# Both value projections of a layer as one matrix product of seven half-size products, with retention's values parked in memory

## The chip, the cores and the metric

The kernel runs on one core of one Trainium2 chip. The metric is device time in microseconds (us) of one execution; three runs of the kernel before took 1214.03 to 1214.75 us, median 1214.11 us.

## The reference

An encoder of two layers over 512 tokens of width 1024. Only the first half of a layer is touched by the change:

```python
h = rms_norm(x, attn_norm_g[l])
proj = h @ w_in[l]
rq, rk, rv, rg, dq, dk, dv = jnp.split(proj, split_at, axis=-1)      # each 512 x 512
ret = retention_bidir(rq, rk * RET_HEAD_DIM ** -0.5, rv, lg_f, lg_b)  # 8 heads
ret = rms_norm(ret, ret_norm_g[l]) * silu(rg)
da = diff_attention(norm(dq) * DIFF_HEAD_DIM ** -0.5, norm(dk), dv, lam, slopes)   # 4 heads
da = rms_norm(da, diff_norm_g[l]) * (1.0 - lam_init)
x = x + concat(ret, da) @ w_out[l]
h = rms_norm(x, ffn_norm_g[l])
x = x + (silu(h @ w_gate[l]) * (h @ w_up[l])) @ w_down[l]
```

The value projections are `dv` (for the differential attention) and `rv` (for retention): together 512 tokens by 1024 columns, summed over 1024 features.

## The kernel before, in words

**Number format.** All products run on 32-bit data rounded for TensorE, in three terms: each operand is a pair hi + lo, and `mm3` (L237 to L239) issues hi·hi, then the two mixed products into one accumulator. Weights come as chunks of 128x1024 (512 KB): SP loads a `raw` tile (three buffers), ScalarE rounds it to `hi` (L224), VectorE subtracts to `lo` (L230). `hi` and `lo` have three buffers each (`NHL`), so the cast of a chunk waits until the matmuls that read the chunk three places earlier are done.

**A layer.** `project_first` makes the first two query and two key tiles. The norm (`Norm.rows`, `Norm.cols`) sums squares on TensorE (L140, L141), makes `rstd` by Ln, Exp (L107), Square (L268) and two VectorE steps (L269, L270), and transposes it with four small matmuls (L301). Then come `project_dv` (four chunks, four token blocks, 96 matmuls of 128x512), the `qk_tile` work of the first tiles, and the four attention heads: scores (L452), a maximum (L456), Exp, the combination of both maps (L464, L465), four transposes on TensorE (L468), the rounding to `ah` (ScalarE, L471) and `al` (VectorE, L472), and the product with `dv` into `o`. Retention follows in `STEPS` (a: `prepare`, b: `scores`, n: `norm`, k, V, v, c: states, values, cross terms), and beside it `project_out`, whose first half copies each bank to an `x` tile on ScalarE (L802) and adds the old x to it with an accumulating DMA from the POOL queue (L803).

**Fillers.** What needs no head is a filler: `project_rk(1)`, `project_rq(1)`, `project_rv` (96 matmuls, its four values chunks in two passes over token halves), then rk and rq 2 and 3, then `project_out`. A "-" in `STEPS` takes one filler step. The instructions of each engine run in the order in which the scheduler of the framework put them, by its own model and by the extra dependencies in the code; an engine never overtakes within its own list.

**The feed-forward half** already uses seven half-size products, with 256 columns moving. It isn't touched.

Of the kernel before, what the change touches and what calls it, by code (L numbers as in the profile page):

```python
# [55 lines left out]
def encoder_kernel(ctx: ExitStack, tc: tile.TileContext, xT, xg, wfirst, wsingle, wvv, wout, wgu, wdn, wds, prm, lam, cst, outT):  # L56
# [63 lines left out]
    xscr = ctx.enter_context(tc.tile_pool(name="dpool", bufs=1, space=bass.MemoryType.DRAM)).tile([KT, P, T], F32, name="xscr")  # L120

# [150 lines left out]
    class Norm:  # L272
# [15 lines left out]
        def rows(self):  # L288
            ps = aux_bank()
            column_sums(ps, consts["ones_r"], self.sum)  # L290
# [58 lines left out]
    def layer(l, n1, h, x_src, first_raw):  # L349


        def project_first():
            banks = [b() for b in (acc_bank, acc_bank, sc_bank, sc_bank)]
            for c in range(4):
                w = [t.rearrange("p (k f) -> p k f", f=512) for t in split_chunk(*first_raw[c], first=l == 0 and c == 0)]
                for k in range(2):
                    kt = 2 * c + k
                    for i, ps in enumerate(banks):
                        mm3(ps, cut(w, slice(None), k, slice(i * P, (i + 1) * P)), h[kt], kt == 0, kt == KT - 1)
            return banks  # L360

        def project(name, m):
            w = [t.rearrange("p (k f) -> p k f", f=P) for t in chunk(wsingle[l, SINGLE.index((name, m))])]
            ps = acc_bank()
            for kt in range(KT):
                mm3(ps, cut(w, slice(None), kt), h[kt], kt == 0, kt == KT - 1)
            return ps

        first = project_first()
        if l == 0:  # L370
            nc.sync.dma_start(cst_sb, cst)
            round_ones()
        rstd = n1.rows()
        if l == 0:
            prepare_small()
        rstdc = n1.cols(rstd)
# [62 lines left out]
        def diff_head(hd, qs, ks, v):  # L439
            q, k = qs[hd], ks[hd]  # L440
            o = None
            for th in range(2):
                ah = tpool.tile([P, 4, C], F32R, tag="ah", name=nm("ah"), bufs=NAH)
                al = tpool.tile([P, 4, C], F32R, tag="ah", name=nm("al"), bufs=NAH)
                for i in (2 * th, 2 * th + 1):
                    z = small("z", 2)
                    pr = []
                    for m in range(2):
                        ps = sc_bank()
                        t = slice(i * P, (i + 1) * P)  # L450
                        for part in range(2):
                            nc.tensor.matmul(ps, q[m][:, t], k[m][part], start=part == 0, stop=part == 1)  # L452
# [23 lines left out]
                for j in range(4):  # L476
                    vv = cut(v[hd // 2][j], slice(None), slice((hd % 2) * P, (hd % 2 + 1) * P))
                    mm3(o[:, th * C : (th + 1) * C], vv, (ah[:, j, :], al[:, j, :]), j == 0, j == 3)
# [147 lines left out]
        def project_dv():  # L626
            banks = [b() for b in (out_bank, out_bank, acc_bank, acc_bank)]
            for c in range(4):
                w = [t.rearrange("p (k f) -> p k f", f=512) for t in chunk(wvv[l, 1, c])]
                for i in ((2, 3, 0, 1) if c == 3 else range(4)):  # L630
                    ps = banks[i]
                    for k in range(2):
                        kt = 2 * c + k
                        mm3(ps, cut(h[kt], slice(None), slice(i * P, (i + 1) * P)), cut(w, slice(None), k), kt == 0, kt == KT - 1)
                yield
            dv[:] = [[tuple(tpool.tile([P, 256], F32R, tag="dv", name=nm("dv"), bufs=16) for _ in range(2)) for _ in range(4)] for _ in range(2)]
            for i in (2, 3, 0, 1):
                ps = banks[i]
                for half in range(2):
                    f = slice(half * 256, (half + 1) * 256)  # L640
                    hi, lo = dv[half][i]
                    nc.scalar.activation(hi, ps[:, f], AF.Copy, scale=rstdc[:, i : i + 1])
                    nc.vector.scalar_tensor_tensor(lo, ps[:, f], rstdc[:, i : i + 1], f32(hi), op0=ALU.mult, op1=ALU.subtract)

        def project_rv():
            w = [None] * 4
            rvt = [[tpool.tile([P, 256], F32, tag="dv", name=nm("rv"), bufs=16) for _ in range(4)] for _ in range(2)]
            for th in range(2):
                banks = [acc_bank() for _ in range(2)]
                for n, c in enumerate(range(4) if th == 0 else range(3, -1, -1)):  # L650
                    if th == 0 or c == 0:
                        w[c] = [t.rearrange("p (k f) -> p k f", f=512) for t in chunk(wvv[l, 0, c])]
                    for i, ps in enumerate(banks):
                        tok = slice((2 * th + i) * P, (2 * th + i + 1) * P)
                        for k in range(2):
                            mm3(ps, cut(h[2 * c + k], slice(None), tok), cut(w[c], slice(None), k), n + k == 0, n + k == 4)
                    if n == 1:
                        yield
                for i, ps in enumerate(banks):
                    for half in range(2):  # L660
                        t = rvt[half][2 * th + i]
                        nc.scalar.activation(t, ps[:, half * 256 : (half + 1) * 256], AF.Copy, scale=rstdc[:, 2 * th + i : 2 * th + i + 1])
                        rv[half].append(t)
                yield
# [57 lines left out]
        us = []  # L722
        for ps in first:
            us.append(big("u"))
            nc.vector.tensor_tensor(us[-1], ps, rstd, op=ALU.mult)
        early_dv = project_dv()
        next(early_dv)
        for i, ((name, m), u) in enumerate(zip(FIRST, us)):
# [4 lines left out]
            next(early_dv, None)  # L733
# [45 lines left out]
        def project_out(half, get, *then):  # L779
# [27 lines left out]

        fill = fillers(
# [396 lines left out]
```

## Time and profile before

| | us |
|---|---|
| median of three runs | 1214.11 |
| profiled execution, its own time | 1214.05 |
| its span in the trace | 1212.3 |
| TensorE busy in the span | 1208.1 |
| VectorE busy | 958.2 |
| ScalarE busy | 746.6 |
| POOL busy | 106.0 |

TensorE works from end to end at the full granted clock (1.00 in all slices). A matmul's listed duration is longer than its step, since they are pipelined; the distance of two starts is what a matmul costs. The value stage of layer 0 lies at about 28 to 52 us of the trace, the heads reach to about 172 us, retention to 250 us; layer 1 repeats this some 600 us later.

### The profile page before, as it was taken

The page shows a single profiled execution, that of the slowest core. Times are in us where ns is not written, and L with a number is a line of the kernel's source. Part 1 is how long each engine was busy: PE and PEld are TensorE (multiplying, and loading weights), DVE is VectorE, ACT ScalarE, POOL GpSimd, SP SyncE. Part 2 cuts the span into 40 slices and gives each one's busy share as a digit, 9 for nine tenths or more (in the row PEclk, how much of TensorE's full clock was granted, in tenths as well). Part 3 has the DMA queues.
Part 4 walks back from the last instruction along what each step waited for, and adds up shares of the span by engine and source line. Part 5 has one row for each costly group of instructions (what it writes and reads, how often), then busy time and mean ns, then how long its engine had stood idle before and what let it go on. Part 6 is the DMA issues. An engine that isn't in the chain of part 4 may idle for free.

```text
span 1212.3 us, 20100 instructions
## 1 busy us (share of the span) xinstructions
PE 1208.1 (100%) x7659; PEld 1081.4 (89%) x7659; DVE 958.2 (79%) x1585; ACT 746.6 (62%) x1300; POOL 106.0 (9%) x124
## 2 busy tenths in 40 slices
PE   9999999999999999999999999999999999999998
PEld 7888888788899999999888888887888999999997
DVE  6899867678978888886648997776789788898763
ACT  6877677565456556655548777774554565665541
POOL 1000001300011111110000000012000011111100
PEclk9999999999999999999999999999999999999999
DMA  7223225933176796782532232469132767867822
GB/s 269 87 79 83 75 92 140 232 98 105 65 169 163 176 215 153 181 220 84 170 113 78 81 80 67 115 151 242 54 122 78 178 145 190 208 160 181 202 79 96
DMA packets 72288, 165.92 MB, mean 137 GB/s; under 512 B 7168, under 2 KB 17664, under 8 KB 72192
## 3 DMA queue, kind: packets, MB, share of 16 engines
q1 hardware_dynamic: 54448, 133.52, 36.2%
q0 software_dynamic: 17312, 30.68, 15.5%
q8 instruction: 60, 0.98, 0.3%
q10 hardware_dynamic: 432, 0.44, 0.1%
q14 instruction: 36, 0.29, 0.1%
HBM read 153.34 MB, written 4.19 MB: 130 GB/s over the span
## 4 chain that ended last, share of the span: by engine, by line
PE 99%; DMA 0%; ACT 0%; DVE 0%; issue 0%
PE acc L945 23%; PE sc L945 17%; PE acc L237 11%; PE acc L238 11%; PE acc L239 11%; PE o L239 3%; PE o L238 3%; PE o L237 3%; PE sc L237 3%; PE sc L239 3%; PE sc L238 3%; PE sc L452 2%; PE sc L601 1%; PE aux L468 1%; PE o L545 1%; PE o L534 1%
## 5 line engine op out<-in xcount | busy, mean ns | idle before, releaser
L224 ACT CAST hi<-raw 128x1024 fp32r<-128x1024 f32 (+2 forms) x117 | 115.9, 994 | 122.5 <-PE acc L238 42.1
L230 DVE TENSOR_TENSOR lo<-raw,hi 128x1024 fp32r<-128x1024 f32 (+2 forms) x118 | 135.0, 1147 | 54.8 <-ACT hi L224 53.4
L239 PE MATMUL acc<-h,lo 128*128 128x512 f32 (+1 forms) x344 | 134.3, 390 | 0.0
L237 PE MATMUL acc<-h,hi 128*128 128x512 f32 (+1 forms) x344 | 134.1, 393 | 0.2
L238 PE MATMUL acc<-h,hi 128*128 128x512 f32 (+1 forms) x344 | 133.8, 389 | 0.0
L945 PE MATMUL acc<-hi,hi 128*128 128x256 f32 x432 | 122.6, 284 | 0.0
L945 PE MATMUL acc<-hi,lo 128*128 128x256 f32 x432 | 122.3, 283 | 0.0
L945 PE MATMUL acc<-lo,hi 128*128 128x256 f32 x432 | 122.3, 283 | 0.0
L902 DVE TENSOR_TENSOR lo<-s,hi 128x1024 fp32r<-128x1024 f32 (+1 forms) x78 | 88.7, 1137 | 32.7 <-ACT hi L901 32.5
L902 DVE TENSOR_TENSOR lo<-raw,hi 128x1024 fp32r<-128x1024 f32 (+1 forms) x78 | 88.8, 1139 | 31.0 <-ACT hi L901 27.2
L901 ACT CAST hi<-s 128x1024 fp32r<-128x1024 f32 (+1 forms) x78 | 76.6, 983 | 51.6 <-PE acc L945 37.2
L901 ACT CAST hi<-raw 128x1024 fp32r<-128x1024 f32 (+1 forms) x78 | 76.5, 981 | 39.0 <-PE acc L945 18.8
L945 PEld LDWEIGHTS acc<-lo,hi 128*128 128x128 f32 x432 | 82.9, 192 | 0.1
L945 PEld LDWEIGHTS acc<-hi,hi 128*128 128x128 f32 x432 | 82.9, 192 | 0.1
L945 PEld LDWEIGHTS acc<-hi,lo 128*128 128x128 f32 x432 | 82.9, 192 | 0.0
L923 POOL DMA_DIRECT2D s<-in_wgu x36 | 43.3, 1204 | 424.3 <-DMA s<-in_wgu 253.5
L237 PEld LDWEIGHTS acc<-h,hi 128*128 128x128 f32 x344 | 64.6, 188 | 14.3 <-PE o L239 0.6
L239 PEld LDWEIGHTS acc<-h,lo 128*128 128x128 f32 x344 | 64.7, 188 | 13.2
L238 PEld LDWEIGHTS acc<-h,hi 128*128 128x128 f32 x344 | 64.6, 188 | 13.2
L945 PE MATMUL sc<-b,s 128*128 128x256 f32 x480 | 69.4, 283 | 0.0
L945 PEld LDWEIGHTS sc<-b,s 128*128 128x128 f32 x480 | 62.8, 192 | 0.0
L945 PE MATMUL acc<-h,hi 128*128 128x256 f32 x288 | 53.7, 283 | 0.0
(282 smaller groups left out, 3530.1 us busy)
## 6 DMA issues: line engine op xcount, KB each, us to landing
s<-in_wgu SPq DMA_DIRECT2D x54, 512.0 KB, 5.4
s<-in_wgu POOLq DMA_DIRECT2D x36, 512.0 KB, 7.9
raw<-in_wgu SPq DMA_DIRECT2D x34, 512.0 KB, 5.2
raw<-in_wsingle SPq DMA_DIRECT2D x32, 512.0 KB, 3.5
raw<-in_wvv SPq DMA_DIRECT2D x18, 512.0 KB, 3.5
raw<-in_wgu SPq DMA_DIRECT2D x36, 256.0 KB, 3.9
s<-in_wds SPq DMA_DIRECT2D x24, 384.0 KB, 3.5
raw<-in_wout SPq DMA_DIRECT2D x16, 512.0 KB, 4.4
```

The costliest lines, as they stand in the source:

```text
L224: c = nc.scalar.copy(hi[:, s], raw[:, s])
L230: nc.vector.tensor_tensor(lo[:, s], raw[:, s], f32(hi[:, s]), op=ALU.subtract)
L237: first = nc.tensor.matmul(out, L[0], R[0], start=start, stop=False)
L238: nc.tensor.matmul(out, L[0], R[1], start=False, stop=False)
L239: nc.tensor.matmul(out, L[1], R[0], start=False, stop=stop)
L452: nc.tensor.matmul(ps, q[m][:, t], k[m][part], start=part == 0, stop=part == 1)
L468: nc.tensor.transpose(tp[:, j * P : (j + 1) * P], a[:, j * P : (j + 1) * P], ident)
L534: ins.append(nc.tensor.matmul(o[b, t], r[:, d, b], qw[:, t], start=False, stop=d == 0, skip_group_check=True).ins)
L901: last_cast[0] = nc.scalar.copy(hi, raw).ins.name
L902: last_split[0] = nc.vector.tensor_tensor(lo, raw, f32(hi), op=ALU.subtract).ins.name
L923: nc.gpsimd.dma_start(sums, blocks[:, 0::3], accum_op=ALU.add)
L945: mm = nc.tensor.matmul(ps[:, t], L[x1], R[x2], start=start and k + i == 0, stop=k == n // P - 1 and i == 2, skip_group_check=True)
```

## The change

`[dv|rv]` is treated as one product. Its three dimensions (features, tokens, the two groups of 512 columns) are halved, and seven products of halves take the place of eight. Each of the seven is two token blocks by four feature tiles by three terms: 24 matmuls of 128x512.

- The sums and differences of `h` (`first_sides`, `second_sides`, `last_sides`) are made by ScalarE and VectorE; the first are placed between `rsqrt` and `newton` of the norm. The sums of weights are made by accumulating DMAs from the POOL queue (`summed`, ten in a layer, 512 KB each), into two `sum` tiles and into `raw` tiles that SP has loaded.
- All seven products stand ahead of the heads and between the first `qk_tile` calls. `dv` stays in its tiles. `rv` goes to memory (`spilled`, four writes of 256 KB in a layer), and `load_values` brings it back in eight loads of 128 KB to the tiles of `dv`, which come free during the heads.
- `project_rv` is gone from the fillers, with four "-" of `STEPS`. `BEHIND` ties the rk and rq fillers 2 and 3 behind scores and products of the last head.
- The sums of squares of the norm are issued ahead of the last chunk of `project_first`.
- The first four x copies of `project_out`'s first half move from ScalarE to VectorE.

```diff
-STEPS = "a0 h - b0 - a1 b1 - - - - - - a2 - - a3 b2 !k0+k1+V0+v1+c0+c1+k2+k3 b3 n0 n1 - - - !V2+v3+c2+c3 n2 - - - n3"
+STEPS = "a0 h - b0 - a1 b1 - - a2 - - a3 b2 - - !k0+k1+V0+v1+c0+c1+k2+k3 b3 n0 n1 - - - !V2+v3+c2+c3 n2 - - - n3"
+BEHIND = {'rk2': 's3.0', 'rq2': 's3.1', 'rk3': 's3.3', 'rq3': 'o3.1'}
...
+        def rows(self, between=None):
+            if between is None:
+                self.sums()
+            ps = self.ps
             r = big("rstd", tag="rstd", bufs=1)
             rsqrt(r, ps, 1.0 / D)
+            if between:
+                between()
             newton(r, ps, 1.0 / D, big("nt"))
...
             for c in range(4):
+                if c == 3:
+                    n1.sums()
...
+        def first_sides():
+            for i, d in enumerate(sides):
+                d.update(b11=cut(h[i], slice(None), H1), b21=cut(h[i + 4], slice(None), H1), b22=cut(h[i + 4], slice(None), H2))
+                b1 = d["b1"] = scaled_x(i, "mix", NMIX)
+                nc.vector.tensor_tensor(b1[:, H1], b1[:, H1], b1[:, H2], op=ALU.subtract)
+                d["ta"] = [big(n, F32R, "mix", NMIX) for n in ("hi", "lo")]
+                d["t1"] = split_to(b1[:, H1], cut(d["ta"], slice(None), H1))
...
+            def summed(t, v, c):
+                nc.gpsimd.dma_start(t, wvv[l, v, c], accum_op=ALU.add)
...
+            def product(ps, r, left, start=False):
+                for c in range(2):
+                    w = [t.rearrange("p (k f) -> p k f", f=512) for t in left(c)]
+                    for i in range(2):
+                        for k in range(2):
+                            L, R = cut(sides[2 * c + k][r], slice(None), slice(i * P, (i + 1) * P)), cut(w, slice(None), k)
+                            for n, (x1, x2) in enumerate(((0, 0), (0, 1), (1, 0))):
+                                nc.tensor.matmul(ps[i], L[x1], R[x2], start=start and c + k + n == 0, stop=c + k == 2 and n == 2, skip_group_check=True)
...
+            def pair_sum(v, other, half):
+                def left(c):
+                    new = load_chunk(wvv[l, v, c])
+                    summed(new[0], other, 2 * half + c)
+                    return split_chunk(*new)
...
+            s1, s3 = pair_sum(0, 0, 1), pair_sum(0, 1, 0)
...
+            product(pa, "b11", loaded(1, 0), True)
+            for c in range(2):
+                nc.sync.dma_start(held[c], wvv[l, 0, c])
+                summed(held[c], 0, 2 + c)
+                summed(held[c], 1, c)
...
+            product(pb, "b21", loaded(1, 1), True)
...
+            product(pa, "t2", s2)
...
+            product(pb, "t1", s1, True)
+            last_sides()
...
+            product(pa, "t3", s3)
...
+            product(pb, "b22", s4)
...
+            product(pa, "t4", loaded(0, 1))
...
+        def load_values():
+            for half in range(2):
+                for i in range(4):
+                    t = tpool.tile([P, 256], F32, tag="dv", name=nm("rv"), bufs=16)
+                    nc.sync.dma_start(t, rvscr[l, i][:, half * 256 : (half + 1) * 256])
...
-                    nc.scalar.copy(x[m], ps[m])
+                    (nc.vector.tensor_copy if m < 4 else nc.scalar.copy)(x[m], ps[m])
...
-            [project_rk(1), project_rq(1), project_rv(), project_rk(2), project_rq(2), project_rk(3), project_rq(3), project_out(0, acc_bank, None, None, None)]
+            [project_rk(1), project_rq(1), project_rk(2), project_rq(2), project_rk(3), project_rq(3), project_out(0, acc_bank, None, None, None)]
```

**How the order moves, first place: TensorE at the norm of layer 0.** `aux` with `rstd` is the transpose of the norm, `o` and `acc` are accumulators of the value products; the second fence is the kernel after. Before, the sums end 36 matmuls ahead of the transposes, and the last of them are these:

```order
L239 MATMUL o_392<-hi_505,h_142 128x512
L237 MATMUL o_392<-hi_505,h_152 128x512
L238 MATMUL o_392<-lo_506,h_152 128x512
L239 MATMUL o_392<-hi_505,h_152 128x512
L301 MATMUL aux_376<-cst_sb,rstd_321 128x128 x4
L237 MATMUL acc_393<-hi_397,h_102 128x512
L238 MATMUL acc_393<-lo_398,h_102 128x512
```

After, the last matmul of the sums is L144:

```order
L144 MATMUL aux_286<-lo_288,ones_r 128x512
L708 MATMUL o_445<-hi_452,h_113 128x512
L708 MATMUL o_444<-hi_470,h_124 128x512
L708 MATMUL o_445<-hi_470,h_124 128x512
...
L708 MATMUL o_445<-lo_471,h_134 128x512
L708 MATMUL o_445<-hi_470,h_134 128x512
L311 MATMUL aux_368<-cst_sb,rstd_324 128x128 x4
L708 MATMUL acc_446<-hi_518,h_145 128x512
L708 MATMUL acc_446<-lo_519,h_145 128x512
```

Thirteen matmuls now stand between the sums and the transposes, and the accumulator `acc_446` right behind them is a bank of `project_first` that VectorE must have read.

**Second place: VectorE and POOL in the value stage of layer 0, after only** (before has no such rows). `raw_625` and `raw_729` share a buffer; they are the first chunk of the sum for product t1 and the second for t3. VectorE:

```order
L259 TENSOR_TENSOR lo_666<-b_328,hi_665 128x512
L233 TENSOR_TENSOR lo_629<-raw_625,hi_628 128x1024
L389 TENSOR_TENSOR dv_493<-part_508,dv_492 128x256
L259 TENSOR_TENSOR lo_600<-sq_597,hi_599 128x512
L259 TENSOR_TENSOR lo_672<-b_335,hi_671 128x512
```

POOL:

```order
L699 DMA raw_625<-in_wvv 128x1024
L699 DMA raw_644<-in_wvv 128x1024
L699 DMA sum_448<-in_wvv 128x1024
L699 DMA raw_710<-in_wvv 128x1024
L699 DMA sum_449<-in_wvv 128x1024
L699 DMA raw_729<-in_wvv 128x1024
```

Before, POOL had only fills of tiles up to the heads; after, ten accumulating loads stand there.

**Third place: TensorE at the end of the last head of layer 0.** `aux` are the four transposes of a combined map, `o` with `ah` and `al` the product with `dv`, `acc` the filler (before `project_rv`, after `project_rk(3)`). Before:

```order
L468 MATMUL aux_1598<-cst_sb,sc_1581 128x128 x4
L239 MATMUL acc_1989<-hi_1932,h_131 128x512
L237 MATMUL o_1526<-ah_1462,dv_619 128x256
L238 MATMUL o_1526<-al_1463,dv_619 128x256
...
L468 MATMUL aux_1659<-cst_sb,sc_1642 128x128 x4
L237 MATMUL acc_1988<-hi_2028,h_102 128x512
L238 MATMUL acc_1988<-lo_2029,h_102 128x512
L239 MATMUL acc_1988<-hi_2028,h_102 128x512
```

After:

```order
L242 MATMUL acc_2263<-h_176,lo_2260 128x512
L534 MATMUL aux_1760<-cst_sb,sc_1742 128x128 x4
L534 MATMUL aux_1839<-cst_sb,sc_1822 128x128 x4
L240 MATMUL o_1767<-ah_1703,dv_500 128x256
L241 MATMUL o_1767<-al_1704,dv_500 128x256
```

and VectorE at that place, after:

```order
L792 SCALAR_TENSOR_TENSOR rk_2256<-acc_2263,rstd_324 128x512
L526 RECIPROCAL rz_1894<-z_1879 128x2
L528 TENSOR_SCALAR c_1896<-rz_1894,prm_sb 128x1
L233 TENSOR_TENSOR lo_2566<-raw_2563,hi_2565 128x1024
L530 TENSOR_SCALAR sc_1890<-sc_1890,c_1896 128x512
L538 TENSOR_TENSOR al_1704<-aux_1760,ah_1703 128x4x128
L538 TENSOR_TENSOR al_1817<-aux_1839,ah_1816 128x4x128
```

No filler stands between the last transposes and the products that read them any more, and `al_1704` stands behind a chunk's `lo_2566`, whose `hi_2565` has the buffer that `acc_2263` reads.

## Rows read from the trace of the kernel before

**Rows 1.** The page: span, and busy time of each engine (share, instructions).

```profile
span 1212.3 us, 20100 instructions
...
PE 1208.1 (100%) x7659; PEld 1081.4 (89%) x7659; DVE 958.2 (79%) x1585; ACT 746.6 (62%) x1300; POOL 106.0 (9%) x124
```

**Rows 2.** Waits of TensorE: line, releaser, us in total, times, longest.

```profile
PE aux L118 <- PEq L1197: 0.8, 1, 0.8
```

**Rows 3.** Stretches: length and PE, PEld, DVE, ACT, POOL busy, clock, DMA share, GB/s.

```profile
20.00:40.00 20.00, 20.00 (x92) 16.53 (x91) 11.36 (x28) 9.27 (x16) 0.00 (x0) 1.00 0.36 117
40.00:60.00 20.00, 20.00 (x89) 16.26 (x88) 18.31 (x29) 19.38 (x34) 0.00 (x0) 1.00 0.34 106
60.00:80.00 20.00, 19.96 (x92) 15.87 (x91) 19.74 (x43) 14.93 (x32) 0.00 (x0) 1.00 0.26 79
80.00:100.00 20.00, 20.00 (x107) 16.98 (x106) 19.83 (x41) 15.90 (x30) 3.00 (x5) 1.00 0.25 67
...
160.00:180.00 20.00, 20.00 (x109) 17.19 (x108) 14.51 (x26) 14.35 (x28) 0.00 (x0) 1.00 0.35 105
180.00:200.00 20.00, 20.00 (x102) 16.84 (x101) 16.53 (x25) 16.39 (x28) 2.09 (x4) 1.00 0.48 127
```

**Rows 4.** TensorE at the norm of layer 0: start, duration, line, tiles.

```profile
27.79 0.39 PE L141 MATMUL aux<-lo,ones_r 128*128 128x512 f32 x1
28.02 0.39 PE L237 MATMUL o<-hi,h 128*128 128x512 f32 x1
...
33.26 0.39 PE L239 MATMUL o<-hi,h 128*128 128x512 f32 x1
```

**Rows 5.** VectorE at the same place, the last step of the norm.

```profile
31.29 0.69 DVE L270 SCALAR_TENSOR_TENSOR rstd<-nt,rstd 128x512 f32<-128x512 f32 x1
```

**Rows 6.** Groups by shape: count, busy us, mean ns of one, idle before it.

```profile
L230 DVE TENSOR_TENSOR lo<-raw,hi 128x1024 fp32r<-128x1024 f32 x94 | 114.5, 1220 | 49.5 <-ACT hi L224 48.2 <-PE aux L141 0.5
L224 ACT CAST hi<-raw 128x1024 fp32r<-128x1024 f32 x94 | 98.5, 1050 | 100.3 <-PE acc L238 39.3 <-PE sc L238 38.6 <-PE acc L239 8.7
L465 DVE SCALAR_TENSOR_TENSOR sc<-sc,rz,sc 128x512 f32<-128x512 f32 x32 | 23.9, 746 | 0.5
L472 DVE TENSOR_TENSOR al<-aux,ah 128x512 fp32r<-128x512 f32 x32 | 21.7, 684 | 0.5 <-ACT ah L471 0.4
L960 DVE TENSOR_TENSOR u<-u,acc 128x256 f32<-128x256 f32 x52 | 21.6, 416 | 10.7 <-PE acc L945 9.6 <-ACT b L895 0.8
L471 ACT CAST ah<-aux 128x512 fp32r<-128x512 f32 x32 | 18.4, 583 | 12.2 <-PE aux L468 12.2
L464 DVE TENSOR_SCALAR sc<-sc,c 128x512 f32<-128x512 f32 x32 | 15.4, 482 | 0.5
```

**Rows 7.** DMA issues of the whole span: queue, count, KB each, median us to landing.

```profile
s<-in_wgu SPq DMA_DIRECT2D x54, 512.0 KB, 5.4
s<-in_wgu POOLq DMA_DIRECT2D x36, 512.0 KB, 7.9
...
raw<-in_wvv SPq DMA_DIRECT2D x18, 512.0 KB, 3.5
...
s<-in_wds POOLq DMA_DIRECT2D x16, 384.0 KB, 5.9
```

**Rows 8.** The same for the stretch 200 to 260 us, where DMA is busiest.

```profile
s<-in_wgu POOLq DMA_DIRECT2D x3, 512.0 KB, 9.3
```

**Rows 9.** TensorE at the end of the last head.

```profile
164.96 0.60 PE L468 MATMUL aux<-cst_sb,sc 128*128 128x128 f32 x4
165.31 0.47 PE L237 MATMUL acc<-hi,h 128*128 128x512 f32 x1
...
169.94 0.27 PE L237 MATMUL o<-ah,dv 128*128 128x256 f32 x1
170.06 0.28 PE L238 MATMUL o<-al,dv 128*128 128x256 f32 x1
```

**Rows 10.** VectorE there: the rounding of those transposes.

```profile
166.44 0.68 DVE L472 TENSOR_TENSOR al<-aux,ah 128x512 fp32r<-128x512 f32 x1
```

**Rows 11.** One line: the x copies of `project_out` (duration ns min/median/max, then first and last start).

```profile
L802 ACT COPY x<-acc x16: 565/579/591, 206.2 to 841.1; 128x512 f32<-128x512 f32 x16
```

More of the change, by code (lines that the diff above doesn't have):

```diff
@@ L365, in project, with split_to @@
             for kt in range(KT):
-                mm3(ps, cut(w, slice(None), kt), h[kt], kt == 0, kt == KT - 1)
-            return ps
+                i = mm3(ps, cut(w, slice(None), kt), h[kt], kt == 0, kt == KT - 1)
+                behind = BEHIND.get(name + str(m))
+                if behind and kt == 0:
+                    tc.add_manual_dep(i, marks[behind], order, reason="behind the heads")
+            return ps
+        def split_to(src, dst):
+            hi, lo = dst
+            nc.scalar.copy(hi, src)
+            nc.vector.tensor_tensor(lo, src, f32(hi), op=ALU.subtract)
+            return hi, lo
@@ L369, in layer @@
+        if l == 0:
+            round_ones()
         first = project_first()
@@ L371, in layer @@
             nc.sync.dma_start(cst_sb, cst)
-            round_ones()
-        rstd = n1.rows()
+        rstd = n1.rows(first_sides)
+        us = []
+        for ps in first:
+            us.append(big("u"))
+            nc.vector.tensor_tensor(us[-1], ps, rstd, op=ALU.mult)
+        rstdc = n1.cols(rstd)
+        second_sides()
         if l == 0:
             prepare_small()
-        rstdc = n1.cols(rstd)
         lg, nlgb, lamn, gq, gd, wk, rs = (consts[k] for k in ("lg", "nlgb", "lamn", "gq", "gd", "wk", "rs"))
@@ L624, in layer, with project_values, loaded, s2 @@
         rks, rqs, gates = [], [], []
[L626 to L638, printed above, removed]
+        def project_values():
+            pa, pb = [out_bank() for _ in range(2)], [acc_bank() for _ in range(2)]
+            held = [tpool.tile([P, 1024], F32, tag="ah", name=nm("sum"), bufs=NAH) for _ in range(2)]
+            def summed(t, v, c):
[8 more added lines that the diff above has]
+                                nc.tensor.matmul(ps[i], L[x1], R[x2], start=start and c + k + n == 0, stop=c + k == 2 and n == 2, skip_group_check=True)
+            def loaded(v, half):
+                return lambda c: chunk(wvv[l, v, 2 * half + c])
+            def s2(c):
+                parts = split_chunk(held[c], 1024, 1)
+                summed(held[c], 1, 2 + c)
+                return parts
+            def s4(c):
+                return split_chunk(held[c], 1024, 1)
+            def pair_sum(v, other, half):
[3 more added lines that the diff above has]
+                    return split_chunk(*new)
+                return left
+            s1, s3 = pair_sum(0, 0, 1), pair_sum(0, 1, 0)
+            def col(t, i):
+                return t[:, i : i + 1]
+            def kept(i, t):
@@ L639, in project_dv @@
                 for half in range(2):
                     f = slice(half * 256, (half + 1) * 256)
[L641 to L664, printed above, removed]
@@ L721, in layer @@
         q, k = [None] * 4, [None] * 4
[L722 to L727, printed above, removed]
+        rstdn = small("rstdn", 4)
+        nc.vector.tensor_scalar(rstdn, rstdc, -1.0, None, op0=ALU.mult)
+        values_ahead = project_values()
+        for _ in range(3):
+            next(values_ahead)
         for i, ((name, m), u) in enumerate(zip(FIRST, us)):
@@ L1114, in encoder_kernel @@
             raws = [load_chunk(wfirst[l, c]) for c in range(4)]
-        n, h = layer(l, n, h, xT if l == 0 else xscr, raws)
+        n, h, x = layer(l, n, h, x, xT if l == 0 else xscr, raws)
 def _constants():
```

84 lines of the change are left out of this document (70 added, 14 removed).

## The prediction, made before the changed kernel ran

> **What bounds the kernel now.** I read the page first, then the waits of TensorE, then the stretches, then single rows at the places where the change moves work. The page says that TensorE is busy 1208.1 of 1212.3 us, VectorE 79% and ScalarE 62% [rows 1]. The list of waits has one entry for TensorE, 0.8 us at the start [rows 2], and the stretches show it 20.00 of 20 us busy nearly everywhere, at granted clock 1.00 [rows 3]. So the end is set by the count of TensorE's work alone, and nothing else costs anything today. That has two sides: each matmul that goes is worth its full step, and each wait that the change puts into TensorE's list costs its full length, as there is no idle time that it could take the place of. Second, VectorE is not idle where it matters: 18.31 of 20 us from 40 to 60, 19.74 and 19.83 from 60 to 100 [rows 3]. It has slack at 20 to 40 (11.36) and from 160 on (14.51). A wait that VectorE meets in the value stage is therefore handed to the heads.
>
> **What it removes.** A value projection is 4 chunks x 2 feature tiles x 4 token blocks x 3 terms = 96 matmuls, two of them 192 in a layer; seven products are 7 x 24 = 168. In two layers 48 matmuls of 128x512 go. Their step: 23 matmuls lie between the starts 28.02 and 33.26, so 0.228 us [rows 4]. 48 x 0.228 = 10.9 us, all of it on the path. No other TensorE work changes in count.
>
> **What it adds off TensorE.** Counted over the program, VectorE gets 10 more instructions of 128x1024, 8 of 128x512 and 8 x copies, 12 of three operands with 512, and 48 of 128x256. At 1.220, 0.684, 0.746 and 0.416 us [rows 6] and 0.48 to 0.68 for a copy that has no row on this engine (between L464 and L472), that is 12.2 + 5.5 + 4.6 + 9.0 + 20.0 = 51 us, 25 in a layer. In the value stage the room is 20 - 11.36 + 20 - 18.31 = 10.3 us [rows 3], plus what `project_rv` leaves in the heads (five casts' `lo`, 6.1 us a layer). Twenty accumulating DMAs come to POOL, which is idle there. The spills and reloads of rv go by SP: 8 loads of 128 KB, needed only at about 215 us, long after head 1 frees their tiles; I cost them at nothing, since a landing of a few us is hidden behind heads 2 and 3, and without that cover one landing, 3.5 to 5.4 us [rows 7], would show.
>
> **A, the value stage of layer 0.** First the norm. From the last matmul of the sums (27.79) to the end of `rstd` (31.29 + 0.69 = 31.98) took 4.2 us [rows 4, 5], hidden behind 36 matmuls. After, 13 stand there: 0.23 + 13 x 0.228 = 3.2 us. ScalarE now has a chunk's cast within the chain (up to 1.05 us [rows 6]), so the chain is 4.2 to 5.2 us and the wait 1.0 to 2.0; I take 1.5. Right behind the transposes, `acc_446` needs VectorE to have read `project_first`'s banks, and VectorE does a `lo` of 1.22 and two reads of 0.68 after `rstd`, against 0.4 us of transposes; and by `lo_580` VectorE has some 11 to 12 us of work from `rstd` on, TensorE 39 matmuls and the transposes, 9.3 us. Together a backlog of 0 to 3 us; I take 2.0. Last, product t3: `raw_729` may be loaded only when `lo_629` has read its buffer, then POOL adds to it, then ScalarE casts it. A load is 3.5 us, the accumulating one 5.9 (384 KB, quiet) to 7.9 [rows 7], the cast 1.05: 10.5 to 12.5 us. TensorE has 37 matmuls between the first use of `lo_629` and that of `raw_729`'s `hi`, 8.4 us, and `lo_629` is finished shortly before its use: a wait of 2 to 4 us, none if its accumulating load lands as a plain one does (3.5). I take 3.0, nearer to the quiet end as the DMA share here is 0.36 [rows 3]. A = 6.5 us (0 to 9).
>
> For such loads the Trainium skill ("SBUF — State Buffer", section "SBUF: two separate sides") warns that a DMA issued from GpSimd has its descriptors written by GpSimd, that some instructions of VectorE keep it from writing them, and advises the other queues. The trace agrees in sign: 7.9 us from POOL against 5.4 from SP for the same 512 KB of `in_wgu` [rows 7], though the first also adds. By the SP figure the wait for t3 would be under 2 us and the time some 3 us less; with a stronger lock it is the last rival below.
>
> **C, the value stage of layer 1.** The chain of t3 is the same; the norm's sums come earlier and VectorE is not behind. 0 to 4 us, I take 2.0.
>
> **B, the end of the heads, twice.** Before, the transposes at 164.96 were read by the product at 169.94, and the `al` in between was finished at 167.12 [rows 9, 10]: 17 filler matmuls and another head's transposes covered it. After, `rk3` is behind the last scores and `rq3` behind the last product, and nothing is left. From the end of `acc_2263` the path is: ScalarE's cast `hi_2565`, which needs `acc_2263`'s buffer (1.05), VectorE's `lo_2566` (1.22), L530 (0.48), `al_1704` (0.68) [rows 6] = 3.4 us, or 3.2 with the small overlaps of starts. TensorE has eight small transposes and one product meanwhile: four take 0.35 us from start to start (164.96 to 165.31) [rows 9], so 0.7 + 0.1, and a tail of some 0.2. Wait 2.3. The second half-product then waits for `aux_1900`, `ah_1816` (0.58) and `al_1817` (0.68), 1.3 us against about 0.6 of other work: 0.7. B = 3.0 a layer, 6.0 in all (4 to 7).
>
> **D, retention, twice.** The x copy took 0.579 us on ScalarE [rows 11] and now stands in VectorE's list behind score masks and `lo` parts (16.53 of 20 us busy at 180 to 200 [rows 3]). The third accumulator of `project_out` waits for it, with three matmuls between: bounded by 0.3 (the copy at once) and 2.7 (four instructions of 0.68 ahead). I take 1.7 a layer, 3.4 in all.
>
> **The heads themselves** (72 to 160 us) I cost at 0, up to 2: VectorE has about 1 us of slack against TensorE there, and fewer chunks to split.
>
> **Sum.** 6.5 + 2.0 + 6.0 + 3.4 = 17.9 us of new waits against 10.9 us of matmuls gone: +7.0 us on the profiled execution of 1214.05 us, 1221.0 us. The median of the runs, 1214.11, is the same to 0.1.
>
> **The rivals.**
> *The cover holds.* Accumulating loads land like plain ones, the norm's chain stays at 4.2 us and only B's first waits stay (4.6 us): 1214.05 - 10.9 + 4.6 + 2 (half of D and the norm's) = 1209.8 us, and 1203.2 if no wait at all appears. For it: VectorE's slack at 20 to 40 us and POOL idle [rows 3]. Against it: the three chains above are longer than the TensorE work that stands beside them by rows of this trace. 30%.
> *The waits equal the gain.* A and C at half, B and D as above: 4.3 + 9.4 = 13.7, or D at its low end, 10.9: about 1214 to 1216. 15%.
> *Late sums* (slower still). The ten accumulating loads of a layer take 9.3 us each, as three did in the stretch where DMA is busiest [rows 8], and the two-step `sum` tiles come late too. Against my 5.9 to 7.9, the t3 chain grows by 2.4 us in each layer and the products t2 and b22 by up to as much for one of them: 1221 + 2 x 2.4 + 2.4 = 1228 us. It decides from a landing of about 8 us on. 12%.
> *The change does not do what it says:* the list of TensorE has 48 fewer matmuls of 128x512, so this can only be lost, not absent. No chance is kept for it.
> *Forecast as above,* 43%.
>
> **How the numbers follow.** About 0.2% (2.4 us) is what a measurement of this kernel can tell from no change. Faster (below 1211.7) is the first rival, 0.30; within 0.2% the second, 0.15; slower is the forecast and the late sums, 0.55. The likeliest single case is 1221.0, its own range 1217 to 1225. The range for 8 in 10 goes from 1206 (most of the first rival) to 1228 (the late sums); outside of it I leave about one in ten on each side.
>
> **What would show it.** In the profile of the changed kernel TensorE's list of waits should no longer be empty: entries at the transposes L311 and the first `acc` of L708 in layer 0, for the cast of the second t3 chunk at about 55 to 60 us behind a DMA, at `o` L241 behind `al` L538 near the end of the heads in both layers (2 to 3 us each), and at the first products of `project_out` behind the VectorE copy L927. TensorE's busy time should fall by about 11 us. The accumulating loads of `in_wvv` should land in 6 to 8 us. I am wrong if the waits sum to less than 10.9 us, which needs the t3 chain and the end of the heads both covered, or if VectorE turns out to run behind through all heads, which would show as waits of scores and `aux` between 70 and 160 us that I have at nothing.

## The result, and the profile after

The changed kernel takes 1246.36 us (1245.15 to 1246.71), the kernel before 1214.11: a ratio of 1.0263 (95% interval 1.0248 to 1.0278), 32.3 us slower. The prediction had the sign but not the size: 1221, with a range to 1228. Since 10.9 us of matmuls did go, about 43 us came back, against 17.9 forecast.

The page of the changed kernel (span, engines, granted clock in 40 slices) answers to [rows 1]:

```profile
span 1244.6 us, 20240 instructions
...
PE 1214.3 (98%) x7611; PEld 1079.9 (87%) x7611; DVE 1002.5 (81%) x1673; ACT 772.6 (62%) x1342; POOL 122.9 (10%) x144
...
PEclk9889999999999999999999999999999999999999
```

48 matmuls fewer, and yet more busy time on TensorE: some of them ran slower, among others where the clock's digit is an 8, in the slices of some 31 us at the value stage of layer 0. The waits of TensorE, one line in [rows 2], are now these (line, releaser, us in total, times, longest):

```profile
PE o L708 <- ACT hi L227: 10.4, 2, 5.2
PE acc L240 <- DVE x L927: 3.2, 2, 1.6
PE acc L708 <- DVE u L437: 3.2, 1, 3.2
PE o L241 <- DVE al L538: 2.9, 2, 1.5
PE o L240 <- ACT ah L537: 1.9, 4, 0.7
PE aux L311 <- issue: 1.8, 1, 1.8
...
```

They are the waits that the prediction named, at the places that it named; what is left out is 0.8 us or less a line. What it lacked is in TensorE's own rows at the norm of layer 0 (start, duration, line, tiles, idle before):

```profile
33.12 0.39 PE L708 MATMUL o<-hi,h 128*128 128x512 f32 x1
35.29 0.63 PE L311 MATMUL aux<-cst_sb,rstd 128*128 128x128 f32 x4 [1.78 <-issue]
39.08 0.77 PE L708 MATMUL acc<-hi,h 128*128 128x512 f32 x1 [3.16 <-DVE u L437]
...
43.48 0.63 PE L708 MATMUL acc<-lo,h 128*128 128x512 f32 x1
43.91 1.05 PE L708 MATMUL acc<-hi,h 128*128 128x512 f32 x2
44.76 0.45 PE L708 MATMUL acc<-lo,h 128*128 128x512 f32 x1
45.05 0.62 PE L708 MATMUL acc<-hi,h 128*128 128x512 f32 x2
```

From 33.12 to 39.08 lie 6.0 us for 0.7 us of work. Then 14 matmuls take from 39.08 to 45.05, 0.43 us each instead of 0.228: 2.8 us more. The longer of the two waits is for a bank read (`u`) on VectorE, which stands behind the `lo` of a summed chunk; ScalarE could not cast that chunk before its accumulating load had landed (ScalarE, then VectorE):

```profile
36.03 1.04 ACT L227 CAST hi<-sum 128x1024 fp32r<-128x1024 f32 x1 [2.29 <-DMA sum<-in_wvv]
...
37.11 1.22 DVE L233 TENSOR_TENSOR lo<-sum,hi 128x1024 fp32r<-128x1024 f32 x1 [1.92 <-ACT hi L227]
38.25 1.28 DVE L437 TENSOR_TENSOR u<-acc,rstd 128x512 f32<-128x512 f32 x2
```

Stretches of 2 us (length, TensorE busy, granted clock, DMA share, GB/s) say why the matmuls behind it are slow:

```profile
36.00:38.00 2.00, 0.00 (x0) 1.00 1.03 240
38.00:40.00 2.00, 0.92 (x2) 0.51 1.06 281
40.00:42.00 2.00, 2.00 (x6) 0.50 1.07 286
...
44.00:46.00 2.00, 2.00 (x9) 0.78 1.09 216
46.00:48.00 2.00, 2.00 (x10) 1.00 1.04 205
```

TensorE stood idle, and when it began again the granted clock was 0.50, the 1.2 GHz level, until some 6 us later. So this wait cost its length and then the slow matmuls behind it. The Trainium skill ("TensorE: Matmul & The Clock Gate", section "HAM oscillation — how this bites in real kernels") describes this of kernels that wait between bursts; the trace agrees, with 0.50 behind the two waits of 1.8 and 3.2 us here and behind one wait of 5.2 us at t3 in each layer.

By the distance of successive starts against the same distance before, the loss lies so: norm of layer 0, 5.3 us of waits and 2.8 of slow matmuls; product t3 in layer 0, 5.4 and 2.4; t3 in layer 1, 5.3 and 2.9; end of the heads 5.3 and 4.8 in all in the two layers; retention 3.9 and 3.8. That is 41.9 us of the 43.

The chain of t3 in layer 0, from the rows of SP, POOL, ScalarE and TensorE: the buffer comes free at 53.2, SP loads, POOL adds from 58.59, ScalarE casts at 66.29.

```profile
53.21 5.41 SPq L203 DMA_DIRECT2D raw<-in_wvv  x3
...
58.59 0.86 POOL L699 DMA_DIRECT2D raw<-in_wvv  x1 [6.77 <-DVE lo L233]
...
61.79 0.40 PE L144 MATMUL aux<-lo,bones_r 128*128 128x512 f32 x1
...
66.29 1.04 ACT L227 CAST hi<-raw 128x1024 fp32r<-128x1024 f32 x1 [5.76 <-DMA raw<-in_wvv]
...
67.38 1.22 PE L708 MATMUL o<-hi,hi 128*128 128x512 f32 x2 [5.20 <-ACT hi L227]
```

From the start of the load (the first of the three in that row) to that of the accumulating load are 5.4 us, and from there to the cast 7.7, where I had 3.5 and 5.9 to 7.9; in layer 1 it is 8.6 and 5.5. The landings in the first 75 us (queue, count, KB, median us):

```profile
raw<-in_wvv SPq DMA_DIRECT2D x10, 512.0 KB, 7.3
sum<-in_wvv POOLq DMA_DIRECT2D x6, 512.0 KB, 8.7
...
raw<-in_wvv POOLq DMA_DIRECT2D x4, 512.0 KB, 8.5
sum<-in_wvv SPq DMA_DIRECT2D x2, 512.0 KB, 8.0
```

Before, the same plain chunks landed in 3.5 us [rows 7]; the DMA share, 0.36 from 20 to 40 us before [rows 3], is above 1.0 in all the stretches shown from 36 to 48 us. The loads collide with each other: in the run without accumulating loads, below, the same ten plain chunks landed in 3.8 us.

### The profile page after: what moved, and what is told of

The parts are those of the page before. It is cut to its first block, busy times and chain, and to the rows that moved or that the text cites. A ratio compares the mean times of both kernels' runs of the same rounds, so it can differ in the third digit from the quotient of the medians.

```text
span 1244.6 us, 20240 instructions
## 1 busy us (share of the span) xinstructions
PE 1214.3 (98%) x7611; PEld 1079.9 (87%) x7611; DVE 1002.5 (81%) x1673; ACT 772.6 (62%) x1342; POOL 122.9 (10%) x144
## 4 chain that ended last, share of the span: by engine, by line
PE 86%; DMA 5%; DVE 5%; ACT 3%; issue 1%; SPq 0%; ACTq 0%; POOLq 0%; DVEq 0%
PE acc L1065 22%; PE sc L1065 17%; PE acc L240 7%; PE acc L242 7%; PE acc L241 7%; DMA raw<-in_wvv 3%; PE o L241 3%; PE o L242 3%; PE o L240 3%; PE sc L240 3%; PE sc L241 2%; PE sc L242 2%; PE sc L517 2%; PE o L708 2%; DVE lo L233 2%; PE o L611 1%
## 5 line engine op out<-in xcount | busy, mean ns | idle before, releaser
L233 DVE TENSOR_TENSOR lo<-raw,hi 128x1024 fp32r<-128x1024 f32 (+2 forms) x120 | 137.6, 1149 | 37.9 <-ACT hi L227 37.0
L1022 DVE TENSOR_TENSOR lo<-s,hi 128x1024 fp32r<-128x1024 f32 (+1 forms) x78 | 88.9, 1139 | 32.3 <-ACT hi L1021 32.1
```

The lines of the kernel that those rows point to most:

```text
L233: nc.vector.tensor_tensor(lo[:, s], raw[:, s], f32(hi[:, s]), op=ALU.subtract)
L1022: last_split[0] = nc.vector.tensor_tensor(lo, raw, f32(hi), op=ALU.subtract).ins.name
```

## The experiments

**Keeping TensorE busy in the t3 waits.** The edit, in `product`:

```diff
+                    if r == "t3" and c == 1:
+                        wb = sc_bank()
+                        for n in range(24):
+                            held_mm = nc.tensor.matmul(wb, warm[0], warm[1], start=True, stop=True).ins
+                            tc.add_manual_dep(held_mm, last.name, order, reason="keep busy")
+                            last = held_mm
...
```

> The changed kernel, with 24 matmuls of ones (128x512, result unused) put on TensorE in each layer where it waits for the second summed chunk of product t3. They take the place of idle time (5.2 us each) and change no operand. Theory (the granted clock falls because TensorE stood idle, and the matmuls behind a wait then run at half speed for some us): the waits stay, now filled, and the 2.4 and 2.9 us of slow matmuls behind them vanish: about 5 us less than the changed kernel, 1241 us. Rival (these matmuls are slow for another reason of that place, such as the DMA traffic): no change, 1246 us.

1245.55 us (1244.52 to 1247.07): no gain that can be told. Yet the theory on the clock held where it was tested: behind the filled wait the stretch that was at 0.50 is at full clock,

```profile
68.00:70.00 2.00, 2.00 (x10) 1.00 0.45 180
70.00:72.00 2.00, 2.00 (x10) 1.00 0.00 0
```

and the 2.4 and 2.9 us of slow matmuls are gone there. The gain did not last: the feed-forward half of layer 0 begins only 1.4 us earlier than in the changed kernel. The waits of that run show where it went: TensorE now waits for VectorE's maxima in the heads, and for the key tiles of retention's second pair, neither of which the changed kernel's list has at that length:

```profile
PE sc L667 <- DMA khi<-khi: 3.2, 1, 3.2
PE sc L667 <- DVE arg L656: 3.1, 1, 3.1
PE sc L517 <- DVE mx L522: 2.3, 3, 1.3
```

That was the first sign that something else bounds the heads and retention. It is not proof: the scheduler also ordered the work behind the edit anew (the first scores of layer 0 start at 79.3 us, in the changed kernel at 94.4), and what the new order itself costs was not separated, here or in the runs below.

**Leaving out the sums of weights.**

```diff
             def summed(t, v, c):
-                nc.gpsimd.dma_start(t, wvv[l, v, c], accum_op=ALU.add)
+                return
```

> The changed kernel without the accumulating DMAs: the weight chunks are loaded and used unsummed, so four of the seven products get the wrong weights; the count of matmuls, casts and plain loads is the same. Theory (the waits of the value stage are the landing times of accumulating loads): both t3 waits go with the slow matmuls behind them, 5.4 + 2.4 + 5.3 + 2.9 = 16 us, and of the norm's 8.1 us some 5: 1225 us (1222 to 1229). Rival (VectorE's backlog and the plain loads make them): at most 8 us less, 1238 us or more.

1238.4 us (1236.16 to 1239.4), just the rival's figure. The t3 waits did go, and the value stage of layer 1 has none left. The plain loads of the first 75 us landed in about half the time:

```profile
raw<-in_wvv SPq DMA_DIRECT2D x10, 512.0 KB, 3.8
```

But in layer 0 the first scores came 13.6 us earlier than in the changed kernel and the feed-forward half only 1.6 us earlier. Scores inside the heads that now wait for VectorE (0.9 and 2.2 us), the end of the heads, the `arg` and `khi` waits of 3.1 and 3.2 us and slow matmuls behind them took the rest.

**A buffer of its own for t3.**

```diff
-                    new = load_chunk(wvv[l, v, c])
+                    if other == v:
+                        new = load_chunk(wvv[l, v, c])
+                    else:
+                        new = (tpool.tile([P, 1024], F32, tag="ah", name=nm("third"), bufs=NAH), 1024, 1)
+                        load_piece(new, wvv[l, v, c], 0)
```

> The changed kernel, with the two chunks for product t3 loaded into two tiles that stand free until the heads, so that the load does not wait until VectorE has read a raw buffer; the accumulating DMAs stay. Theory (the chain is long because the load starts so late: buffer, load, accumulate, cast): both t3 waits and their slow matmuls go, 16 us: 1230 us. Rival (an accumulating load of 8 us behind others on POOL is enough for the wait): less than half of it, 1239 us or more.

1237.32 us (1234.3 to 1238.65), between the two. In layer 1 the wait vanished, as the theory said. In layer 0 it was replaced by one of 8.2 us: t3's loads, now early, took their place on POOL and DMA ahead of others, ScalarE waited for each summed chunk in turn, and product t2 waited for a copy that stands behind them in ScalarE's list:

```profile
PE o L708 <- ACT part L755: 8.2, 1, 8.2
```

**al ahead of the chunk at the end of the heads.** The cast and `lo` of output-projection chunks after the first got an order behind `ah` and `al` of the last head:

```diff
-                    w[m] = w[m + 1] = [t.rearrange("p (k f) -> p k f", f=256) for t in chunk(wout[l, half, m // 2])]
+                    w[m] = w[m + 1] = [t.rearrange("p (k f) -> p k f", f=256) for t in chunk(wout[l, half, m // 2], after=marks["ah"] if half == 0 and m else None, behind=marks["al"] if half == 0 and m else None)]
```

> The changed kernel, with the cast and the subtraction of the second output-projection chunk tied behind the rounding of the last head's maps, so that al stands ahead of the chunk's lo in VectorE's list. Theory (the chunk that waits for a weight buffer stands in front of al): the 5.3 and 4.8 us lost at the end of the heads fall to about 2 each: 1240 us. Rival (the transposes and the copy ah alone need that long without a filler): at most 2 us less, 1244 us.

1244.9 us (1243.42 to 1247.16): no gain that can be told. The place itself went from 5.3 and 4.8 us to 3.2 in both layers, but retention then lost 3.4 us and more at the second pair's scores, instead of 1.6 at the x copy. The two lists differ there: in the changed kernel twelve matmuls of `acc` stand between the x copy's wait and that score, here the score stands ahead of them (first the changed kernel, then this run):

```profile
227.83 0.28 PE L667 MATMUL sc<-q,khi 128*128 128x256 f32 x1
...
224.26 0.36 PE L670 MATMUL sc<-q,khi 128*128 128x256 f32 x1 [3.16 <-DMA khi<-khi]
```

**All four repairs** (the two above, all x copies on ScalarE, and the two bank reads `u` tied ahead of the summed chunk's `lo` in VectorE's list):

```diff
-                parts = split_chunk(held[c], 1024, 1)
+                parts = split_chunk(held[c], 1024, 1, behind=banks_read if c == 0 else None)
...
-                    (nc.vector.tensor_copy if m < 4 else nc.scalar.copy)(x[m], ps[m])
+                    nc.scalar.copy(x[m], ps[m])
```

> The changed kernel with four repairs at once: product t3's chunks in their own tiles, the two bank reads of the norm ahead of the summed chunk's lo in VectorE's list, al ahead of the output-projection chunk at the end of the heads, all x copies on ScalarE. Theory A (after the first four runs: with the rv filler out of the heads VectorE's list is nearly the bound from the value stage to the end of the heads, so time saved early is given back as waits behind VectorE later): 1230 us or more, hardly under the best single repair. Theory B (the waits are separate and add up): 16 + 5 + 6 + 4 us less, 1216 us.

1234.49 us (1232.47 to 1235.86): 12 us less than the change, not 31. The waits are not separate. The value stage of layer 1 has no wait any more, but that of layer 0 still has the one that came with the buffer of its own:

```profile
PE o L713 <- ACT part L760: 7.8, 1, 7.8
```

By the distances of starts that stage lost 8.9 us, against 15.9 in the changed kernel; and retention, where waits of 3.2 and 3.1 us stand at the second pair's scores, lost more than in the changed kernel instead of less.

**The move alone.** `project_values` with 2 x 96 matmuls as before, all ahead of the heads; `first_sides` and `second_sides` not called:

```diff
+            for v in (1, 0):
+                banks = [b() for b in (out_bank, out_bank, acc_bank, acc_bank)]
+                for c in range(4):
+                    w = [t.rearrange("p (k f) -> p k f", f=512) for t in chunk(wvv[l, v, c])]
...
+                            mm3(banks[i], cut(h[kt], slice(None), slice(i * P, (i + 1) * P)), cut(w, slice(None), k), kt == 0, kt == KT - 1)
...
+                        nc.sync.dma_start(rvscr[l, i], t)
```

> The move alone: all of the changed kernel but the seven products; both value projections as 2 x 96 matmuls as before, both ahead of the heads, rv written to memory and loaded back, the same fillers, pins and x copies; no weight sums and no sums of h. Theory A (taking the rv filler out of heads and retention costs by itself): 5 us at the end of the heads and 4 us in retention in each layer stay: about 1232 us. Theory B (the sums make the loss, the move is free): 1214 to 1218 us.

1231.07 us (1229.55 to 1233.76): the move costs 17.0 us without one of the sums. It holds all that comes with the move: rv's way through memory, the ties of the fillers and the x copies on VectorE, which by themselves cost nothing in the kernel before (a run below). Its value stage has a single wait of 0.7 us. What it lost is in retention, where `STEPS` had four "-" more:

```profile
PE sc L666 <- DMA khi<-khi: 3.6, 1, 3.6
PE sc L666 <- DVE arg L655: 3.3, 1, 3.3
...
```

and, behind the one of them in layer 0 (3.3 us), matmuls at half clock again:

```profile
208.00:210.00 2.00, 0.15 (x1) 1.00 0.59 131
210.00:212.00 2.00, 0.59 (x2) 0.54 0.90 195
212.00:214.00 2.00, 2.00 (x6) 0.50 0.76 93
```

The copies that make the key tiles (`khi`) are not slow: they landed in 2.3 us around the wait of layer 0, in 5.4 us from 200 to 212 us in the kernel before, which does not wait for them. They are issued late, behind ScalarE's and VectorE's work for that pair.

**Seven products with nothing added.** No accumulating loads, and plain `h` in place of its sums:

```diff
+                d.update(t1=cut(h[i], slice(None), H2), t2=cut(h[i + 4], slice(None), H2), t3=cut(h[i], slice(None), H2), t4=cut(h[i], slice(None), H1))
```

> The changed kernel without accumulating DMAs and without the sums and differences of h: the seven products read plain chunks and plain h, so their values are wrong; 168 matmuls a layer, none of the extra VectorE, ScalarE and POOL work of the sums. Theory A (the extra VectorE work ahead of the heads keeps VectorE late through them): well below the 1238 us without accumulating DMAs alone, by most of the 10 us of VectorE work that goes in each layer: 1220 to 1226 us. Theory B (the VectorE work of the sums lies beside other work): 1236 to 1238 us.

1223.5 us (1222.47 to 1227.25). Against the move alone that is 7.6 us less for 10.9 us of matmuls (the single times of the two kernels spread over 4 and 5 us); against the run without accumulating loads it is 14.9 us less, for the VectorE and ScalarE work of the sums of `h` alone.

**The x copies alone**, in the kernel before:

```diff
-                    nc.scalar.copy(x[m], ps[m])
+                    (nc.vector.tensor_copy if m < 4 else nc.scalar.copy)(x[m], ps[m])
```

> The kernel before, with one edit of the change alone: the first four x copies of the output projection's first half on VectorE. Theory A (VectorE's list makes the copy late for the accumulator): 1.6 to 2 us a layer, 1217 to 1218 us. Theory B (only in the changed kernel, whose retention has no filler in front of it): 1214 us.

1215.03 us, ratio 1.0007 (0.9998 to 1.0017): no difference that can be told, and no new wait. So the move of these copies does not make them late by itself. In the changed kernel, which waits for them, no filler stands in front; that this is the reason was argued, not tested alone.

**Layer 1 alone**, with the four repairs; layer 0 is the kernel before's (its `project_dv`, `project_rv` and `STEPS` put back for that layer):

```diff
-        values_ahead = project_values()
-        for _ in range(3):
+        if l:
+            rstdn = small("rstdn", 4)
+            nc.vector.tensor_scalar(rstdn, rstdc, -1.0, None, op0=ALU.mult)
+            values_ahead = project_values()
+            for _ in range(3):
+                next(values_ahead)
+        else:
+            values_ahead = project_dv()
             next(values_ahead)
```

> Layer 0 as in the kernel before; the change, with the four repairs of the run with all four, in layer 1 alone. Theory A (each layer pays for itself; layer 1 of that run lost 19.8 - 15.1 = 4.7 us more than layer 0 had): 1219 us (1218 to 1220). Theory B (layer 1 loses because layer 0 leaves VectorE and the DMA queues late): the 5.5 us of matmuls come through at least in half, 1212 us or less.

1219.16 us (1.0039, 1.0026 to 1.0051). The value stage of layer 1 has no wait at all, as in the run with the buffer of its own; from 600 to 690 us the accumulating loads landed in 5.4 to 5.8 us and the plain ones in 3.5. The same repairs left 7.8 us in layer 0, whose loads fall together with those of the start. So 5.5 us of matmuls are gone in that layer and 10.4 us are lost between the end of the heads and the second norm.

**One filler moved into retention**, behind a mark set at its first scores; first in the kernel with layer 1 alone, then in the move alone:

```diff
-BEHIND = {'rk2': 's3.0', 'rq2': 's3.1', 'rk3': 's3.3', 'rq3': 'o3.1'}
+BEHIND = {'rk2': 's3.0', 'rq2': 's3.1', 'rk3': 's3.3', 'rq3': 'r0'}
...
+                marks[f'r{pr}'] = i.ins.name
```

> The run before it, with one edit: the filler rq3 is tied behind the first scores of retention instead of behind the last head's product, so that its 24 matmuls (5.4 us) can stand where TensorE waits 3.3 us for the key tiles of the second pair and then runs 1.8 us slow. Theory A (retention waits because nothing is left to fill it): 4 to 5 us less, 1214 us. Theory B (the filler is then missing at the end of the heads and what is won is lost there): 1218 to 1219 us.

> The move alone (both value projections ahead of the heads in 2 x 96 matmuls, rv through memory), with the same edit: rq3 behind the first scores of retention. Theory A (the 17 us that the move costs are mostly the missing filler in retention: waits of 3.4 and 3.8 us and slow matmuls of 2.6 us): 9 us less, 1222 us. Theory B (the filler is only taken from another place that needs it): 1229 us or more.

1220.49 and 1232.64 us, against 1219.16 and 1231.07: no gain in either. Retention's wait went, and one of the same size came at the end of the heads, which the filler had covered, here in the move alone:

```profile
PE aux L143 <- ACT hi L258: 8.7, 2, 4.4
PE sc L666 <- DMA khi<-khi: 1.3, 2, 0.8
```

**The last two fillers cut in halves**, layer 1 alone: 12 matmuls of rk3 behind the last head's transposes (first the third, then the second of them), 12 of rq3 behind retention's first scores:

```diff
+                if behind and kt == 4 and name + str(m) == "rk3":
+                    tc.add_manual_dep(i, marks["t3.2"], order, reason="behind the transposes")
+                if behind and kt == 4 and name + str(m) == "rq3":
+                    tc.add_manual_dep(i, marks["r0"], order, reason="behind the first scores")
```

> The change in layer 1 alone with the four repairs, and its last two fillers cut in halves: 12 matmuls of rk3 tied behind the last head's third transposes, and 12 of rq3 behind the first scores of retention. Layer 1 lost 3.2 us at the end of the heads and 3.4 + 1.9 + 1.9 us in retention with the fillers whole. Theory A (each place needs a part only, so halves of 2.7 us cover more than wholes): about 5 us less than with whole fillers, 1213 to 1215 us, the kernel before's time. Theory B (the work missing from there is conserved, halves only shift the wait): 1218 to 1220 us.

> The run with split fillers, with one edit: the second half of rk3 is tied behind the last head's second transposes instead of the third, ahead of the product that in that run waits 1.2 us for ah and of the transposes that wait 1.5 us for VectorE. Theory A (what is left of layer 1's loss is where the fillers stand): both waits go, 2 us or more less, 1213 us, under the kernel before. Theory B (VectorE is then the bound, the wait only moves to the next reader): 1215 us.

1215.39 us (ratio 1.0014, 1.0005 to 1.0023), so slower by some 0.1%, then 1214.97 us (1.0005, 0.9996 to 1.0014), no difference from before that can be told. Halves cover more than wholes, 3.8 us of the 5; the 0.4 us of the second move lie within the spread. What is left in the second run is spread, above all over four places:

```profile
PE aux L545 <- DVE sc L542: 1.3, 1, 1.3
PE sc L679 <- DMA khi<-khi: 1.0, 1, 1.0
...
PE acc L244 <- DVE rq L856: 0.7, 1, 0.7
PE o L244 <- ACT ah L548: 0.4, 1, 0.4
```

No version here beats the kernel before.

## Why the prediction was right or wrong, step by step

**What it removes** was right: 48 matmuls are gone. TensorE's busy time was to fall by about 11 us, though, and rose by 6.2. VectorE's added work came to 44 us, against 51 counted. That each matmul is worth its full step does not hold either where it was tried: seven bare products in place of eight gave 7.6 of 10.9 us, in a place where the heads that follow have nothing to fill with.

**The places** were right: transposes L311, `acc` of L708, t3's cast, `al` L538, copy L927, each with the releaser named but the first, which the profile puts to "issue" (`rstd` was finished 0.1 us before it).

**A and C are the step that failed:** the price of the waits in the value stages. A: 6.5 forecast, 15.9 measured. C: 2.0 against 8.2. That is 15.6 of the 24 us by which the new losses (41.9) exceed the forecast (17.9). The prediction priced each wait at its length alone, with the landings of a quieter stage. Of the 24.1 us, 16.0 are the waits themselves, against 8.5: the loads took 5.4 and 7.7 us in t3's chain in layer 0, with medians of 7.3 to 8.7 in the stage, against my 3.5 and 5.9 to 7.9; and in the norm I costed the summed chunk's `lo`, which stands ahead of the bank reads in VectorE's list, but not that its chunk had not landed (a wait of 2.3 us on ScalarE). The norm's own chain was right, 1.8 us against 1.5. The other 8.1 us are the clock, of which the prediction says nothing: matmuls at 0.50 behind the three waits. The rival of late sums had its condition (a landing above 8 us) fulfilled, but its price, 2.4 us a landing, lacked the clock too.

**B and D were right in their waits**, but too low in what the waits cost. The waits listed at the end of the heads in layer 0 are 0.48, 1.47, 0.45 and 0.21, 2.6 us against 3.0, and the x copy's 1.6 against 1.7:

```profile
200.11 0.38 PE L240 MATMUL o<-ah,dv 128*128 128x256 f32 x1 [0.48 <-ACT ah L537]
201.96 0.58 PE L241 MATMUL o<-al,dv 128*128 128x256 f32 x1 [1.47 <-DVE al L538]
...
224.98 0.50 PE L240 MATMUL acc<-hi,hi 128*128 128x512 f32 x1 [1.61 <-DVE x L927]
```

The first cost 5.3 us with what ran slow behind it (and 4.8 in layer 1); and a further 1.9 us a layer was lost later in retention, which I had not looked for. B and D together: 9.4 forecast, 17.8 measured.

**The heads at 0 to 2 us** held in the changed kernel: TensorE is busy in all of the 95 us from 100 to 195, and in layer 1 in all of the 86 us from 714 to 800. It does not hold by itself. I treated the waits as things that stand beside the gain and are subtracted from it. Where the waits of the value stage are gone (layer 1 of the repaired kernels, the bare products) or smaller (without accumulating loads), part of the loss comes back later, in the heads, at their end or in retention. The rv filler, 96 matmuls a layer, was what TensorE did while VectorE and ScalarE worked through heads and retention; the move that takes it out costs 17.0 us by itself. The prediction priced its absence at one place (B) and not in retention. How much of what comes back is due to the missing filler, and how much to the new order that the scheduler gives each kernel, stays open; that the place of the fillers matters is shown by the halves, which gave 3.8 us with the same work.

**The sum as the runs have it**, one after the other: move +17.0 (1231.1), seven products -7.6 (1223.5), sums of `h` +14.9 (1238.4), accumulating loads +8.0 (1246.4). The order matters; each step is measured on top of the one before it, and each of these kernels has its own order of instructions. The third is the difference of two kernels that differ in VectorE's and in ScalarE's part of the sums; which of both engines it is was not separated.

**The first rival**, that the cover holds, had 30% and 1209.8 us. The bare products are its best case, without any sum at all: 1223.5 us. With plain layer 0 and hand-split fillers the change comes to 1215.0. So that chance was too high. (The second rival's own sum, 13.7 - 10.9 us on 1214.05, reaches 1216.9 us and not 1216.)

## What to carry to other kernels

Work that is free to stand anywhere is what hides the latency of the work that isn't: before it is moved ahead, count for each stage that it leaves how long the other engines' chains are and what TensorE still has to do beside them. When TensorE is busy throughout, price a new wait at its length, and look in the trace whether the matmuls behind it run at half clock; here that added about half of the wait's length in the value stage and nothing behind the x copy. And test a saving of matmuls first without what it needs elsewhere (here the bare products and the move alone): two runs told more than the sum over all waits.

## What the runs showed of the hardware that was not expected

The clock did not fall behind every wait, and the length of a wait does not tell. At t3 it was at 0.50 behind 5.2 us, in both layers, and in the norm of layer 0 behind 1.8 and 3.2 us with four transposes between. Behind waits of 1.6 us for the x copy it stayed at 1.00, but at the end of the heads it fell behind waits of only 0.5 and 1.5 us with one matmul between:

```profile
200.00:202.00 2.00, 0.43 (x2) 0.97 0.04 8
202.00:204.00 2.00, 2.00 (x9) 0.50 0.73 254
```

In the move alone it fell behind a wait of 3.3 us in layer 0 (2.6 us of slow matmuls) and stayed at 1.00 behind one of 3.6 us in layer 1 (0.1 us). The slow time behind a wait was 2.4 to 2.9 us in the value stage.

Accumulating loads from the POOL queue were little slower than plain ones beside them where DMA was full: 8.5 and 8.7 us against 7.3 and 8.0 in the first 75 us. In layer 1 alone, with a DMA share of 0.5 to 0.6, it was 5.4 to 5.8 against 3.5. Both kinds became slower in the full stage; the plain ones were back at 3.8 us when the accumulating ones were left out.

Three edits that each removed a wait seen in the trace (busy TensorE, own buffer, al first) gave 0.8, 9.0 and 1.5 us of the 5, 16 and 6 that the rows promised, the first and the last within the spread of the runs.
